# The first stage of a four-layer encoder: the norm's vectors on SyncE's queue, the third block's split between the squares, the sums over partitions inside group two

## The chip, the cores and the metric

The kernel runs on one core of a Trainium2 chip. The time is the device time of one execution in microseconds (us); lower is better. Engines are named as in the profile: PE (TensorE, matrix multiplications; PEld is its load of weights), DVE (VectorE), ACT (ScalarE), POOL (GpSimd) and SP (SyncE, which here only issues DMAs). L81 is line 81 of the kernel's file.

## The reference

Four layers on a sequence of 256 rows of 1024 numbers. Every layer is two half-step feed-forward networks with a token mixer between them (attention, convolution, Fourier, gated linear attention, one a layer). Only the first feed-forward network is touched by the change:

```python
def _rmsnorm(x, g):
    xf = x.astype(F32)
    y = xf * lax.rsqrt(jnp.mean(xf * xf, axis=-1, keepdims=True) + EPS)
    return (y * g.astype(F32)).astype(x.dtype)

def _swiglu(h, w1, w3, w2):
    return (jax.nn.silu(h @ w1) * (h @ w3)) @ w2

    h = x
    for i in range(DEPTH):
        h = h + 0.5 * _swiglu(_rmsnorm(h, norm_g[i, 0]), ffn_w1[i, 0], ffn_w3[i, 0], ffn_w2[i, 0])
        ...
```

`w1` and `w3` are 1024 x 2816, `w2` is 2816 x 1024, all float32.

## The kernel before

**Layout.** The activations stand transposed: 1024 features on partitions, in four tiles `h0` to `h3` of 128 x 2 x 256 (two groups of 128 features, 256 positions each). The weights come in **blocks** of 1 MB (128 x 2048), in the order in which they are used: block 0 is the first 256 columns of `w1`, block 1 those of `w3`, block 2 the next 256 columns of `w1`, block 3 those of `w3`, and so on. Four `raw` buffers take the loads, four `w` buffers what is made of them.

**Exact products.** Every operand is split into a high part that TensorE takes exactly and a low part. `split_block` (L160) does it for a block: ACT copies `raw` to the high part (L167, 128 x 2048), DVE subtracts (L170), and then the next load is issued into the `raw` buffer that has come free. `split` (L634) does it for smaller pieces (ACT L635, DVE L636). `wide` (`mm` at L81) multiplies: for each of the eight k (128 features) and each half c of the 256 columns a matmul of 256 columns and one of 512. A block used against all of x is so 32 matmuls.

**Groups.** A feed-forward network works through 11 pairs of blocks; I call the 64 matmuls on blocks 0 and 1 **group one**, the 32 on block 2 **group two** and the 32 on block 3 **group three**. `w1` blocks accumulate in two banks of PSUM, PA (`A0`, `A1`), `w3` blocks in two others, PB (`A2`, `A3`). Before a bank may be started anew, what stands in it is read: ACT copies one half (`parts`, L466) and DVE adds the other (`add`, L471). So group two may start only when `sl0`, group one's sum in PA, is read, and group three only when `br0` in PB is read and block 3 is split.

**The norm.** `normed` (L295) multiplies `h` by the gains only (vectors in `cols`, one small load) and splits the result into `x`; the factor 1/sqrt(mean of squares) is applied after the products (`times_r`). For that `square` (L314) sums squares into `acc`: ACT squares each `h` tile (L320, L328; the two `sq` buffers alternate, so the third `sq` waits until DVE has added the first), DVE adds (L355), folds the two halves (L335), and splits the result into `R` high (ACT L340) and low (DVE L341). `stats(True)` (L400) sums over partitions with two matmuls of a matrix of ones (**the sums**), and DVE makes the reciprocal root: L410, then L367, L368 and three Newton steps of L371 to L373, given out one after the other by `steps.pop(0)()`.

**Order.** Nothing is scheduled automatically: each engine executes its instructions in the order of the code, and waits on semaphores where it needs another engine's result. In `setup` (L196) POOL issues the load of `cols`; SP issues, for each j, the load of `h` tile j and of slice j of blocks 0 and 1, then blocks 2 and 3 and a small constant. At most eight loads of SP are outstanding, since their semaphores are reused. Then ACT and DVE make x and the splits slice by slice, then come the four `square` calls, the last of which calls `split_block` for block 2 after the fold. The first network (`first` in `ffn`) alternates between PA and PB, two k at a time, in all of group one, then makes the sums, then group two.

Of the kernel before, what the change touches and what calls it, by code (L numbers as in the profile page):

```python
# [38 lines left out]
class Enc:  # L39
# [156 lines left out]
    def setup(self):  # L196
        nc, a = self.nc, self.a
        self.perm = self.stages[0][1] == 0
        cols = self.const.tile([128, sum(n for _, n in COLS)], F32, name="cols")
        nc.gpsimd.dma_start(cols, a["cols"])  # L200
        names = [(*k, c) for k, n in COLS for c in range(n)]
        self.cols = {k if k[0] == "n" else (k[0], k[-1]): (cols, i) for i, k in enumerate(names)}

        self.h = [self.hp.tile([128, 2, 256], F32, name=f"h{j}") for j in range(4)]
        first = range(2 if self.stages[0][0] == "ffn" else 0)
        for b in first:
            self.raw[b] = self.sb(self.wp, [128, 2048], F32, "raw", NR)
            self.wsp[b] = self.pair(self.wp, [128, 2048], "w", NW)
        self.ndma = self.nsplit = len(first)
        for j in range(4):  # L210
            nc.sync.dma_start(self.h[j], a["x"][j])
            s = slice(512 * j, 512 * j + 512)
            for b in first:
                nc.sync.dma_start(self.raw[b][:, s], self.blocks[b][2][:, s])
        while self.ndma < NR:
            self.dma_block()
        self.ident = self.const.tile([128, 128], F32, name="ident")
        nc.sync.dma_start(self.ident, a["c_ident"])
        st = self.open_stage()
        one = self.sb(self.ev, [128, 128], F32, "one")  # L220
        nc.vector.memset(one, 1.0)
        self.ones_r = self.const.tile([128, 128], F32R, name="ones")
        nc.gpsimd.tensor_copy(self.ones_r, one)
        nc.scalar.activation(one[:, 0:1], one[:, 0:1], AF.Copy)
        self.ones = f32(self.ones_r)
        self.acc = self.hp.tile([128, 2, 256], F32, name="acc")
        self.begin_close()
        for j in range(4):
            self.normed(j)
            s = slice(512 * j, 512 * j + 512)  # L230
            for b in first:
                self.split(self.raw[b][:, s], self.wsp[b][:, :, s])
        for b in first:
            del self.raw[b]
        while self.ndma < NR + len(first):
            self.dma_block()
        for j in range(4):
            self.square(j, before_split=self.split_block)
        self.pend = NW - self.nsplit
        self.close_stage(st)  # L240

# [69 lines left out]
            nc.vector.tensor_scalar(y[:, 1], h[:, 1], g[1], None, ALU.mult)  # L311
            self.xn[j] = y

    def square(self, j, h=None, before_split=None):  # L314

        nc = self.nc
        h = self.h[j] if h is None else h
# [14 lines left out]
        if j == 3:  # L332
            self.flush_acc()
            if self.row_norm():
                nc.vector.tensor_tensor(self.acc[:, 0], self.acc[:, 0], self.acc[:, 1], ALU.add)  # L335
            if before_split:
                before_split()
            if self.row_norm():
                hi, lo = self.nsq = [self.sb(self.hp, [128, 256], F32R, "R", 2) for _ in range(2)]
                nc.scalar.activation(hi, self.acc[:, 0], AF.Copy)  # L340
                nc.vector.tensor_tensor(lo, self.acc[:, 0], f32(hi), ALU.subtract)  # L341
# [101 lines left out]
    def ffn(self, l, s):  # L443
        nc = self.nc
# [6 lines left out]
        PA, PB = (self.two(up_half, n) for n in range(2))  # L451

        def up(w, P, ks=range(8)):
            for k in ks:
                for c in range(2):
                    self.wide(P, c, w[:, :, :, 128 * c:128 * c + 128], k, self.xk(k), k == 0, k == 7)

        def take_up(n, i, P):
            up(self.take((n, i)), P)
            self.done()  # L460
# [23 lines left out]

        first = self.nstage == 0
        wa, wb = self.take(("w1", 0)), self.take(("w3", 0))
        cuts = [range(2 * n, 2 * n + 2) for n in range(4)] if first else [range(4), range(4, 8)]
        for n, ks in enumerate(cuts):
            if n == len(cuts) - 1:
                if not first:  # L490
                    self.pump(1)
                up(wa, PA, ks[:2])
                if first:
                    break
                steps = self.stats(True)
                up(wa, PA, ks[2:])
            else:
                up(wa, PA, ks)
                up(wb, PB, ks)
        self.done()  # L500
        sl0 = parts(PA, "sl")
        add(sl0, PA)
        up(wb, PB, ks)
        self.done()
        if first:
            steps = self.stats(True)
        held = self.pend - 2
        steps.pop(0)()
        br0 = parts(PB, "br")
# [3 lines left out]
        steps.pop(0)()  # L513
        self.pump(1)
        for i in range(1, NG):
            take_up("w1", i, PA)
            sl = parts(PA, "sl")
            if i == 1:
                self.pump(1, between=lambda: (add(sl, PA), times_r(sl0), times_r(sl)))
# [34 lines left out]
        w = self.take(("w2",))  # L554
# [8 lines left out]
        for p in range(NP):  # L563
# [3 lines left out]
            w = self.take(("w2", 1, p))  # L567
# [1072 lines left out]
```

## Time and profile before

| | us |
|---|---|
| median of 3 runs | 1934.15 |
| lowest, highest | 1933.92, 1937.98 |
| the profiled execution, its own time | 1937.17 |
| its span (first to last instruction) | 1935.0 |
| PE busy in the span | 1906.1 (99%) |
| DVE busy | 1397.5 (72%) |
| ACT busy | 995.4 (51%) |

The span is what the rows below divide; the time of an execution is some 2 us longer. A busy PE is not one at its peak, but idle time of PE is time in which it waits. The trace's rows give start and duration in us from the span's start; in square brackets stands how long the engine was idle before and whose result ended that.

### The profile page before, as it was taken

The numbers are of one execution on the slowest core, as the hardware profiler recorded it, in microseconds if no ns is written. First come the engines' busy times: TensorE is split into PE (matmuls) and PEld (weight loads), VectorE is DVE, ScalarE is ACT, GpSimd is POOL, SyncE is SP. The second block draws the span as 40 slices with busy tenths as digits, with TensorE's granted clock in tenths as the row PEclk, the third lists the DMA queues.
The fourth block names the chain that finished last, engine by engine and source line by source line (L and its number), as shares of the span: only waits on it lengthen the run. The fifth ranks groups of instructions, "written<-read, shape, count | busy, mean of one in ns | idle before, by whom it ended". The sixth has DMA issues, their size and how long they took to land.

```text
span 1935.0 us, 29203 instructions
## 1 busy us (share of the span) xinstructions
PE 1906.1 (99%) x12272; PEld 1683.3 (87%) x12272; DVE 1397.5 (72%) x1850; ACT 995.4 (51%) x1273; POOL 35.0 (2%) x55
## 2 busy tenths in 40 slices
PE   7999999999999999899999999999999999999998
PEld 6888999888888898788888889988888888998886
DVE  7776567876687767787668776687777766768774
ACT  6554444655455544555545544555445455756452
POOL 0000000000040000000000000000000000000000
PEclk9999999999999999899999999999999999999999
DMA  7655533465445543245545544365546553335550
GB/s 264 219 194 193 188 131 131 153 217 196 174 164 212 194 162 144 79 163 216 196 174 196 195 176 164 133 226 183 183 168 220 201 196 111 131 130 193 199 196 22
DMA packets 48644, 338.10 MB, mean 175 GB/s; under 512 B 5568, under 2 KB 5744, under 8 KB 8192
## 3 DMA queue, kind: packets, MB, share of 16 engines
q1 hardware_dynamic: 47952, 335.11, 48.3%
q8 instruction: 96, 1.57, 0.3%
q0 software_dynamic: 560, 1.12, 0.2%
q14 instruction: 36, 0.29, 0.0%
HBM read 335.16 MB, written 1.05 MB: 174 GB/s over the span
## 4 chain that ended last, share of the span: by engine, by line
PE 92%; DVE 5%; ACT 2%; DMA 1%; issue 1%; SPq 0%; DVEq 0%; ACTq 0%
PE B L81 50%; PE A L81 41%; DVE w L170 1%; ACT w L167 1%; DVE zc L765 1%; DMA raw<-in_ffn_w_dram 0%; PE A L84 0%; DMA h<-in_x_dram 0%; ACT zc L880 0%; PE B L84 0%; DVE h L279 0%; DVE acc L355 0%; DVE x L304 0%; DVE sl L474 0%; ACT x L302 0%
## 5 line engine op out<-in xcount | busy, mean ns | idle before, releaser
L170 DVE TENSOR_TENSOR w<-raw,w 128x2048 fp32r<-128x2048 f32 x315 | 720.4, 2293 | 289.7 <-ACT w L167 289.4
L167 ACT ACTIVATE w<-raw 128x2048 fp32r<-128x2048 f32 x315 | 598.8, 1909 | 109.0 <-PE A L81 47.4
L81 PE MATMUL B<-x,w 128*128 128x256 f32 (+1 forms) x3968 | 643.5, 322 | 1.4 <-DVE sl L471 1.2
L81 PEld LDWEIGHTS B<-x,w 128*128 128x128 f32 x3968 | 571.5, 190 | 71.1 <-issue 5.5
L81 PE MATMUL A<-x,w 128*128 128x256 f32 x3008 | 522.4, 335 | 10.9 <-DVE w L636 7.3
L81 PEld LDWEIGHTS A<-x,w 128*128 128x128 f32 x3008 | 455.5, 189 | 74.9 <-DVE w L636 7.3
L81 PE MATMUL B<-g,w 128*128 128x256 f32 (+1 forms) x1408 | 251.1, 336 | 0.3 <-DVE w L170 0.2
L81 PE MATMUL A<-g,w 128*128 128x256 f32 (+1 forms) x1408 | 250.3, 336 | 0.0
L81 PEld LDWEIGHTS B<-g,w 128*128 128x128 f32 x1408 | 216.5, 187 | 32.2 <-DVE g L636 0.5
L81 PEld LDWEIGHTS A<-g,w 128*128 128x128 f32 x1408 | 216.6, 187 | 31.4
L635 ACT ACTIVATE g<-br 128x512 fp32r<-128x512 f32 x88 | 55.6, 632 | 252.9 <-DVE br L480 252.9
L474 DVE TENSOR_TENSOR sl<-sl,R 128x512 f32<-128x512 f32 x176 | 121.9, 696 | 2.5
L636 DVE TENSOR_TENSOR g<-br,g 128x512 fp32r<-128x512 f32 x88 | 61.1, 695 | 61.4 <-ACT g L635 61.4
L302 ACT ACTIVATE x<-h,cols 128x256 fp32r<-128x256 f32 x88 | 39.9, 501 | 68.3 <-DVE h L279 49.0
L466 ACT ACTIVATE br<-B 128x256 f32<-128x256 f32 x88 | 30.3, 385 | 76.3 <-PE B L81 76.3
L477 ACT ACTIVATE sl<-sl 128x512 f32<-128x512 f32 x88 | 55.0, 627 | 24.5 <-DVE sl L474 24.4
L466 ACT ACTIVATE br<-A 128x256 f32<-128x256 f32 x88 | 30.2, 384 | 71.5 <-PE A L81 71.4
L81 PE MATMUL B<-w,x 128*128 128x256 f32 (+1 forms) x504 | 62.6, 284 | 0.0
L81 PEld LDWEIGHTS B<-w,x 128*128 128x128 f32 x504 | 61.3, 191 | 0.4 <-issue 0.3
L480 DVE TENSOR_TENSOR br<-sl,br 128x512 f32<-128x512 f32 x88 | 60.7, 690 | 0.5
L466 ACT ACTIVATE sl<-A 128x256 f32<-128x256 f32 x88 | 29.8, 377 | 53.1 <-PE A L81 53.1
L466 ACT ACTIVATE sl<-B 128x256 f32<-128x256 f32 x88 | 29.9, 378 | 51.5 <-PE B L81 51.1
(293 smaller groups left out, 1088.9 us busy)
## 6 DMA issues: line engine op xcount, KB each, us to landing
raw<-in_ffn_w_dram SPq DMA_DIRECT2D x262, 1024.0 KB, 4.8
raw<-in_attn_w_qk_dram SPq DMA_DIRECT2D x12, 1024.0 KB, 4.8
raw<-in_conv_w_pw_dram SPq DMA_DIRECT2D x12, 1024.0 KB, 4.8
raw<-in_gla_w_in_dram SPq DMA_DIRECT2D x12, 1024.0 KB, 4.8
raw<-in_attn_w_v_dram SPq DMA_DIRECT2D x6, 1024.0 KB, 4.8
raw<-in_fnet_w_dram SPq DMA_DIRECT2D x4, 1024.0 KB, 4.8
raw<-in_gla_w_o_dram SPq DMA_DIRECT2D x4, 1024.0 KB, 4.7
raw<-in_ffn_w_dram SPq DMA_DIRECT2D x8, 256.0 KB, 6.1
```

What stands on the lines that cost most here:

```text
L81: return self.nc.tensor.matmul(out, lhsT, rhs, start=start, stop=stop, skip_group_check=True)
L167: self.nc.scalar.activation(w[:, 0], raw, AF.Copy)
L170: (eng or self.nc.vector).tensor_tensor(w[:, 1], raw, f32(w[:, 0]), ALU.subtract)
L302: nc.scalar.activation(xh[:, c], h[:, c], AF.Copy, scale=g[c])
L466: nc.scalar.activation(t[:, c], P[c][:, 1], AF.Copy)
L474: nc.vector.tensor_tensor(t, t, self.Rb(), ALU.mult)
L477: nc.scalar.activation(t, t, AF.Silu)
L480: nc.vector.tensor_tensor(br, sl, br, ALU.mult)
L635: self.nc.scalar.activation(p[:, 0], src, AF.Copy)
L636: self.nc.vector.tensor_tensor(p[:, 1], src, f32(p[:, 0]), ALU.subtract)
L765: nc.vector.scalar_tensor_tensor(o, x, w, o, ALU.mult, ALU.add)
```

## The change

Four edits, all in the first stage (the same code serves the other stages, whose order does not change):

- `cols` is loaded by SP, ahead of its other loads, and no longer by POOL.
- `split_block` for block 2 stands between the second and the third `square` call, and no longer in the fourth one.
- In group one, k 0 to 3 still alternate between PA and PB; then come k 4 to 7 of PA in one go, and then those of PB.
- The two matmuls of the sums no longer stand between group one and group two but in the middle of group two, after its first four k.

```diff
--- before.py
+++ after.py
@@ -197,7 +197,7 @@
         nc, a = self.nc, self.a
         self.perm = self.stages[0][1] == 0
         cols = self.const.tile([128, sum(n for _, n in COLS)], F32, name="cols")
-        nc.gpsimd.dma_start(cols, a["cols"])
+        nc.sync.dma_start(cols, a["cols"])
         names = [(*k, c) for k, n in COLS for c in range(n)]
         self.cols = {k if k[0] == "n" else (k[0], k[-1]): (cols, i) for i, k in enumerate(names)}
 
@@ -235,7 +235,9 @@
         while self.ndma < NR + len(first):
             self.dma_block()
         for j in range(4):
-            self.square(j, before_split=self.split_block)
+            if j == 2:
+                self.split_block()
+            self.square(j)
         self.pend = NW - self.nsplit
         self.close_stage(st)
 
@@ -311,7 +313,7 @@
             nc.vector.tensor_scalar(y[:, 1], h[:, 1], g[1], None, ALU.mult)
             self.xn[j] = y
 
-    def square(self, j, h=None, before_split=None):
+    def square(self, j, h=None):
 
         nc = self.nc
         h = self.h[j] if h is None else h
@@ -333,8 +335,6 @@
             self.flush_acc()
             if self.row_norm():
                 nc.vector.tensor_tensor(self.acc[:, 0], self.acc[:, 0], self.acc[:, 1], ALU.add)
-            if before_split:
-                before_split()
             if self.row_norm():
                 hi, lo = self.nsq = [self.sb(self.hp, [128, 256], F32R, "R", 2) for _ in range(2)]
                 nc.scalar.activation(hi, self.acc[:, 0], AF.Copy)
@@ -484,26 +484,28 @@
 
         first = self.nstage == 0
         wa, wb = self.take(("w1", 0)), self.take(("w3", 0))
-        cuts = [range(2 * n, 2 * n + 2) for n in range(4)] if first else [range(4), range(4, 8)]
-        for n, ks in enumerate(cuts):
-            if n == len(cuts) - 1:
-                if not first:
-                    self.pump(1)
-                up(wa, PA, ks[:2])
-                if first:
-                    break
-                steps = self.stats(True)
-                up(wa, PA, ks[2:])
-            else:
-                up(wa, PA, ks)
-                up(wb, PB, ks)
+        if first:
+            for n in range(2):
+                for P, w in ((PA, wa), (PB, wb)):
+                    up(w, P, range(2 * n, 2 * n + 2))
+            up(wa, PA, range(4, 8))
+        else:
+            for P, w in ((PA, wa), (PB, wb)):
+                up(w, P, range(4))
+            self.pump(1)
+            up(wa, PA, range(4, 6))
+            steps = self.stats(True)
+            up(wa, PA, range(6, 8))
         self.done()
         sl0 = parts(PA, "sl")
         add(sl0, PA)
-        up(wb, PB, ks)
+        up(wb, PB, range(4, 8))
         self.done()
         if first:
+            wa = self.take(("w1", 1))
+            up(wa, PA, range(4))
             steps = self.stats(True)
+            up(wa, PA, range(4, 8))
         held = self.pend - 2
         steps.pop(0)()
         br0 = parts(PB, "br")
@@ -513,7 +515,10 @@
         steps.pop(0)()
         self.pump(1)
         for i in range(1, NG):
-            take_up("w1", i, PA)
+            if first and i == 1:
+                self.done()
+            else:
+                take_up("w1", i, PA)
             sl = parts(PA, "sl")
             if i == 1:
                 self.pump(1, between=lambda: (add(sl, PA), times_r(sl0), times_r(sl)))
```

ACT from its first square on, before, then after (`w_167` and `w_159` are block 2, `w_269` and `w_301` block 3, `A_69` and `A_70` the banks of PA, `sl` group one's sum):

```order
L320 ACTIVATE acc<-h_81 128x512
L328 ACTIVATE sq_157<-h_82 128x512
L328 ACTIVATE sq_160<-h_83 128x512
L328 ACTIVATE sq_163<-h_84 128x512
L167 ACTIVATE w_167<-raw_101 128x2048
L340 ACTIVATE R_172<-acc 128x256
L466 ACTIVATE sl_236<-A_69 128x256
```

```order
L322 ACTIVATE acc<-h_81 128x512
L330 ACTIVATE sq_157<-h_82 128x512
L167 ACTIVATE w_159<-raw_101 128x2048
L330 ACTIVATE sq_165<-h_83 128x512
L330 ACTIVATE sq_168<-h_84 128x512
L340 ACTIVATE R_172<-acc 128x256
L466 ACTIVATE sl_228<-A_69 128x256
```

Block 2's copy stands two squares earlier.

DVE from the last slice of block 1 on, before, then after (`B_73` is the bank of the sums):

```order
L636 TENSOR_TENSOR w_88<-raw_87,w_88 128x512
L355 TENSOR_TENSOR acc<-acc,sq_157 128x512
L355 TENSOR_TENSOR acc<-acc,sq_160 128x512
L355 TENSOR_TENSOR acc<-acc,sq_163 128x512
L335 TENSOR_TENSOR acc<-acc 128x256
L170 TENSOR_TENSOR w_167<-raw_101,w_167 128x2048
L341 TENSOR_TENSOR R_173<-acc,R_172 128x256
L471 TENSOR_TENSOR sl_236<-sl_236,A_69 128x256
L471 TENSOR_TENSOR sl_236<-sl_236,A_70 128x256
L410 TENSOR_SCALAR R_249<-B_73 128x256
```

```order
L641 TENSOR_TENSOR w_88<-raw_87,w_88 128x512
L170 TENSOR_TENSOR w_159<-raw_101,w_159 128x2048
L355 TENSOR_TENSOR acc<-acc,sq_157 128x512
L355 TENSOR_TENSOR acc<-acc,sq_165 128x512
L355 TENSOR_TENSOR acc<-acc,sq_168 128x512
L337 TENSOR_TENSOR acc<-acc 128x256
L341 TENSOR_TENSOR R_173<-acc,R_172 128x256
L471 TENSOR_TENSOR sl_228<-sl_228,A_69 128x256
L471 TENSOR_TENSOR sl_228<-sl_228,A_70 128x256
L410 TENSOR_SCALAR R_265<-B_73 128x256
```

Block 2's subtraction has moved from behind the fold to ahead of all three additions; the rows from L341 on stand as before.

PE around the sums, before, then after (`x_9_116` holds k 0 and 1, `x_10_125` k 2 and 3, `x_11_134` k 4 and 5, `x_12_143` k 6 and 7; `w_88` is block 1):

```order
L81 MATMUL A_72<-x_12_143,w_88 128x256
L81 MATMUL A_72<-x_12_143,w_88 128x512
L81 MATMUL B_73<-R_172,ones 128x256
L81 MATMUL B_73<-R_173,ones 128x256
L81 MATMUL A_69<-x_9_116,w_167 128x256
L81 MATMUL A_69<-x_9_116,w_167 128x512
```

```order
L81 MATMUL A_70<-x_10_125,w_159 128x256
L81 MATMUL A_70<-x_10_125,w_159 128x512
L81 MATMUL B_73<-R_172,ones 128x256
L81 MATMUL B_73<-R_173,ones 128x256
L81 MATMUL A_69<-x_11_134,w_159 128x256
L81 MATMUL A_69<-x_11_134,w_159 128x512
```

The sums stand behind the first 16 of group two's 32 matmuls, and group two's first matmul follows group one's last.

## Rows read from the trace of the kernel before

**Rows 1.** The page: busy us (share of span) and instructions of PE

```profile
PE 1906.1 (99%) x12272; PEld 1683.3 (87%) x12272; DVE 1397.5 (72%) x1850; ACT 995.4 (51%) x1273; POOL 35.0 (2%) x55
```

**Rows 2.** Waits of PE, whole span: us in total, times, longest us

```profile
PE A L81 <- DVE w L636: 7.3, 1, 7.3
...
PE B L81 <- DVE R L341: 1.4, 1, 1.4
...
PE A L81 <- DVE w L170: 1.1, 1, 1.1
```

**Rows 3.** Timeline of PE, 0 to 60 us: start, duration, engine, line, what

```profile
7.33 12.97 PE L81 MATMUL A<-x,w 128*128 128x256 f32 x64 [7.33 <-DVE w L636]
...
21.79 0.39 PE L81 MATMUL B<-R,ones 128*128 128x256 f32 x1 [1.38 <-DVE R L341]
22.12 5.82 PE L81 MATMUL A<-x,w 128*128 128x256 f32 x32
29.07 17.22 PE L81 MATMUL A<-x,w 128*128 128x256 f32 x96 [1.13 <-DVE w L170]
```

**Rows 4.** Timeline of DVE, 0 to 60 us

```profile
15.91 2.29 DVE L355 TENSOR_TENSOR acc<-acc,sq 128x512 f32<-128x512 f32 x3 [0.35 <-ACT sq L328]
18.23 0.43 DVE L335 TENSOR_TENSOR acc<-acc 128x256 f32<-128x256 f32 x1
19.11 2.29 DVE L170 TENSOR_TENSOR w<-raw,w 128x2048 fp32r<-128x2048 f32 x1 [0.45 <-ACT w L167]
21.32 0.42 DVE L341 TENSOR_TENSOR R<-acc,R 128x256 fp32r<-128x256 f32 x1
21.66 0.75 DVE L471 TENSOR_TENSOR sl<-sl,A 128x256 f32<-128x256 f32 x2
22.32 0.42 DVE L410 TENSOR_SCALAR R<-B 128x256 f32<-128x256 f32 x1
...
26.73 2.28 DVE L170 TENSOR_TENSOR w<-raw,w 128x2048 fp32r<-128x2048 f32 x1
...
32.40 0.74 DVE L471 TENSOR_TENSOR sl<-sl,A 128x256 f32<-128x256 f32 x2
```

**Rows 5.** Timeline of ACT, 0 to 60 us

```profile
5.12 0.91 ACT L302 ACTIVATE x<-h,cols 128x256 fp32r<-128x256 f32 x2 [2.64 <-DMA cols<-in_cols_dram]
...
15.26 1.14 ACT L328 ACTIVATE sq<-h 128x512 f32<-128x512 f32 x2
16.64 0.63 ACT L328 ACTIVATE sq<-h 128x512 f32<-128x512 f32 x1 [0.24 <-DVE acc L355]
17.17 1.90 ACT L167 ACTIVATE w<-raw 128x2048 fp32r<-128x2048 f32 x1
18.98 0.40 ACT L340 ACTIVATE R<-acc 128x256 fp32r<-128x256 f32 x1
```

**Rows 6.** Timeline of SP's queue, 0 to 10 us: issues of loads

```profile
0.74 0.39 SPq L211 DMA_DIRECT2D h<-in_x_dram  x1
...
7.58 1.72 SPq L158 DMA_DIRECT2D raw<-in_ffn_w_dram  x2
```

**Rows 7.** DMA issues, 0.7 to 1.17 us (first `h`): count, KB, us to landing

```profile
h<-in_x_dram SPq DMA_DIRECT2D x1, 256.0 KB, 2.8
```

**Rows 8.** DMA issues, 1.2 to 1.3 us (first slice of block 0, `cols`)

```profile
raw<-in_ffn_w_dram SPq DMA_DIRECT2D x1, 256.0 KB, 3.1
cols<-in_cols_dram POOLq DMA_DIRECT2D x1, 84.0 KB, 3.8
```

**Rows 9.** DMA issues, 7.5 to 8.0 us (block 2)

```profile
raw<-in_ffn_w_dram SPq DMA_DIRECT2D x1, 1024.0 KB, 9.1
```

**Rows 10.** Busy us (x instructions) PE, PEld, DVE, ACT, POOL; PE's clock, DMA share, GB/s

```profile
8.00:10.00 2.00, 2.00 (x7) 1.67 (x7) 1.63 (x4) 1.36 (x3) 0.00 (x0) 1.00 1.06 398
14.00:16.00 2.00, 2.00 (x13) 1.72 (x12) 0.79 (x2) 1.80 (x4) 0.00 (x0) 1.00 1.03 430
...
812.00:814.00 2.00, 1.64 (x7) 1.44 (x8) 0.76 (x2) 2.00 (x3) 0.00 (x0) 0.65 0.80 328
814.00:816.00 2.00, 2.00 (x11) 2.00 (x11) 1.62 (x1) 2.00 (x2) 0.00 (x0) 0.50 0.31 131
816.00:818.00 2.00, 2.00 (x19) 2.00 (x18) 2.00 (x2) 0.14 (x1) 0.00 (x0) 1.00 0.23 33
```

**Rows 11.** Timeline of PE, 808 to 821 us

```profile
812.29 8.99 PE L81 MATMUL A<-zs,w 128*128 128x256 f32 x58 [2.35 <-ACT zs L635]
```

## The prediction

> **What bounds the kernel now.** I read the page first: PE is busy 99% of the span [rows 1], so time is lost only where PE waits, or runs slowly. The waits of PE over the whole span are few, and three of the longest lie in the stage that the change touches [rows 2]: 7.3 us until the first slice of block 0 is split, 1.4 us until the low part of `R` is there for the sums, 1.1 us until block 3 is split. The timeline of PE places them [rows 3]: group one runs from 7.33 for 12.97 us without a wait, the second matmul of the sums begins at 21.79, group two at 22.12, group three at 29.07, and from there 96 matmuls follow without a gap. What matters is therefore one number: when group three starts. After that PE has no wait in these rows, and every microsecond by which the start moves stays in the time.
>
> Next, who sets these starts. Block 0's loads were there early; what held ACT until 5.12 was `cols` [rows 5], issued by POOL and landed 3.8 us after its issue [rows 8]. DVE's rows show the second and third wait [rows 4]: the subtraction of block 2 occupies it from 19.11 for 2.29 us, then the low part of `R` (21.32), then the two additions that empty PA (from 21.66), and group two starts at 22.12 as the first of them ends: block 2 itself was split by 21.40. The chain L410 to the block-3 subtraction (22.32 to 26.73 + 2.28 = 29.01) is DVE's without a pause, and group three starts at its end. So DVE, not PE, carries this stage between 19 and 29 us, and group three starts 29.07 - 22.32 = 6.75 us after L410.
>
> **cols on SP's queue.** The first `h` lands 2.8 us after its issue at 0.74 [rows 6, 7]. With `cols` ahead of it, it is issued one SP issue (0.39 us [rows 6]) later, and lands at about 3.9 to 4.0; `cols`, a third of its size, lands by then. ACT's first product starts near 4.0 in place of 5.12. Block 0's first slice landed 3.1 us after its issue at about 1.2 [rows 8], so near 4.7 with the same delay, when ACT is through with x. From ACT's 5.12 to PE's 7.33 it is 2.2 us, so PE starts near 6.2: 1.1 us earlier (bounds: 0.7, with one more issue time lost, and 1.2, what 3.9 instead of 5.12 leaves). Group one, without a wait before, then ends near 19.1, if its data keep ahead; with PA's k 4 to 7 in one go the last slice of block 0 is needed 8 matmuls earlier, some 1.4 us (8 x 0.18, below). I cost that at nothing, since a stall there would only use up part of the wait that comes next, and the same wait makes PE's earlier start worth nothing.
>
> Loads behind `cols`: the later ones run with the DMA engines full (share 1.03 to 1.06 [rows 10]), and the bytes are the same, so I take block 2's landing as unchanged: issue 7.58 [rows 6] + 9.1 [rows 9] = 16.7. Ends: 0.4 later (the issue time), 0.8 earlier (where ACT would no longer be waiting). The Trainium skill ("Trainium Kernel Development and Optimization", Key Constraints) says that DMAs of SP, ACT and POOL queues run on the same 16 engines, and that issuing from several only saves the sequencer's issue time. That speaks against this edit: by it the issue time is simply lost, +0.4 us on the sum below.
>
> **Block 2's split between the squares.** ACT is through with the second square at about 15.26 + 0.6 = 15.9 [rows 5], before block 2 is there. So ACT now waits for the load, and behind it are queued two squares, on which `R` rests. Step by step, with durations of rows 4 and 5: the copy 16.7 to 18.6 (1.90); the subtraction to 20.9 (2.29); the first addition to 21.6, upon which the third square may overwrite its buffer; three additions (2.29 with their waits) to 23.2; fold (0.43) 23.6; high part on ACT (0.40) 24.0; low part (0.42) 24.5; the first of the two PA additions (0.75 for two) 24.85. Before, the same addition ended at 22.1. The additions used to run while ACT copied block 2; now DVE stands idle meanwhile (15.91 - 0.35 = 15.6 to 18.6) and does them afterwards. Block 2 is split 0.5 us earlier, which nobody waits for.
>
> **The sums in group two.** Group two follows group one directly in PE's order, but its first matmul starts PA anew, and PA is emptied by `add`, which on DVE stands behind the low part of `R`. So group two starts at 24.85 in place of 22.12, 2.7 later, whatever PE gained at the front. Then 16 matmuls: 17.22/96 = 0.18 each [rows 3], 2.9 us, to 27.75. Only now come the sums. In the old order L410 came 0.53 us after the second of them began; the first adds 0.2 (between its weight load and its length). So L410 starts at 28.4 and not at 22.32: 6.1 later. Group two's other half (2.9) covers part of that for PE, but DVE's chain of 6.75 us to group three is unbroken, the same instructions in the same order. Group three starts at 28.4 + 6.75 = 35.15. **Sum without the clock: +6.1 us.** Behind that nothing changes: PA's next sum `sl` is added on DVE 32.40 - 29.07 = 3.3 us after group three starts [rows 3, 4], within its 5.7 us.
>
> **What the waits do to PE's clock.** PE would idle from 19.1 to 24.85 (5.7 us) and from the end of group two, about 31.1, to 35.15 (4.0 us), in place of 1.4 and 1.1. At 812.29 a wait of 2.35 us ends [rows 11] and the granted clock drops to 0.50, the 1.2 GHz level [rows 10]: 11 matmuls in 2 us there, 19 in the next 2 us at 1.00. At the start too, after 7.33 us of nothing, 7 matmuls lie in 8 to 10 us against 13 in 14 to 16 us, though the column reads 1.00. After the waits of 1.4 and 1.1 us the rates are full: 32 matmuls in 5.82 us right after the first [rows 3]. Both new waits exceed the 2.35 us, so I let both cost a stretch at half clock. The stretch at 812 is some 3.5 us long (0.65 in the first window, of which 1.6 us ran, 0.50 in the second). At 11 to 19 it loses 42%: 1.5 us. I take 1.6 for each; the ends are 0 and 2.4 (all of a group's 5.8 us at the lower rate). The first delays the sums (they stand behind 16 matmuls that run slowly), the second falls on group three, which PE has no slack to regain. The Trainium skill ("TensorE: Matmul & The Clock Gate", Why this matters for your kernels) advises against PE idle gaps above about 3 us between bursts, since the clock then halves. By it too both waits cost, and the second, for which I have only one row, is the likelier; the row at 812 shows a shorter wait doing it.
>
> **Total:** 6.1 + 1.6 + 1.6 = 9.3 us. The profiled execution took 1937.17 us with a span of 1935.0; these become 1946.5 and 1944.3. The median of the runs is 1934.15, 3.0 below the profiled one, so the forecast for a median is 1934.15 + 9.3 = 1943.45, rounded 1943.5.
>
> **Rivals.**
> 1. *One clock drop only* (the second wait ends in full clock): +7.7, 1941.8. For it: the second wait is the shorter, and only one row shows such a drop.
> 2. *No drop*: +6.1, 1940.2; with block 2 landing 0.8 us earlier 1939.4. Against it: the row at 812.
> 3. *Longer slow stretches, later loads*: +0.4 and 2.4 for each drop: 6.1 + 0.4 + 4.8 = 11.3, 1945.5.
> 4. *Faster*: the point that decides is whether PA is emptied by the end of group one, near 19.1. Were the two additions done by then, PE would gain 1.1 at the start and lose both waits, 1.4 and 1.1 [rows 2]: -3.6, 1930.5. For it: PE's order is indeed freed of the wait for `R`, and the sums are no longer between the groups. Against it: DVE's order puts these additions behind L341, which needs all squares, and the last of them cannot be added before 23 us while the copy waits for a load that lands at 16.7.
> 5. *Within the measurement*: the mechanism holds but costs little: the load lands early and no clock drops (1939.4), and the chain of rows 4 runs 1.5 us shorter than its rows say, about 1938. Against it: these rows are back to back, with nothing to save.
>
> **How the numbers follow.** Something like 0.2% (3.9 us) is what a measurement of this kernel can tell from no change; the three runs of before differ by 4.1. Both drops 0.52, one 0.2, none 0.08, longer stretches 0.1, within 0.2% 0.07, faster 0.03. Slower by over 0.2% (above 1938.0) are the first four: 0.90. The forecast is the likeliest case, 1943.5. The range leaves out rivals 4 and 5 and what runs scatter beyond: from 1939.4 (none, load early) to 1946.5 (longer stretches and 1.0 of scatter).
>
> **What the next profile would show.** PE's first matmul near 6.2; group one's end near 19; group two waiting for DVE's L471 (not for the split of block 2) until about 24.9; the sums at 28 to 30; group three waiting for block 3's subtraction until 35 to 37; the granted clock at 0.50 after the first of these waits and probably after the second; from there on every row later by the same amount. I am wrong if group two starts before 22.1, if ACT's copy of block 2 starts much before 16.7, or if L410 runs ahead of group two. An end that is later by about 6 with a clock at 1.00 would mean that only the clock term failed.

## The result, and the profile after

The changed kernel takes 1945.72 us (median of 5 runs, 1943.57 to 1948.5) against 1935.22 us of the kernel before (median of 5 on the same chip, 1933.92 to 1937.98): 1.0054 times as long, with an interval of 1.0043 to 1.0066, or 10.5 us more. The forecast was 1943.5, 9.3 us more. The profiled execution took 1948.5 us with a span of 1946.4.

PE in the first 60 us of the changed kernel; the columns and names are those of [rows 3]:

```profile
6.29 14.06 PE L81 MATMUL A<-x,w 128*128 128x256 f32 x64 [6.29 <-DVE w L641]
25.84 4.45 PE L81 MATMUL A<-x,w 128*128 128x256 f32 x16 [5.49 <-DVE sl L471]
30.13 0.40 PE L81 MATMUL B<-R,ones 128*128 128x256 f32 x2
30.36 2.94 PE L81 MATMUL A<-x,w 128*128 128x256 f32 x16
37.31 19.58 PE L81 MATMUL A<-x,w 128*128 128x256 f32 x96 [4.01 <-DVE w L170]
```

Group one starts 1.0 us earlier than in [rows 3] and ends at the same time: its 64 matmuls take 14.06 and not 12.97 us. Then PE stands for 5.49 us until DVE's L471 has emptied the first bank of PA. The first 16 matmuls of group two take 4.45 us, the next 16 only 2.94. Group three starts at 37.31 (29.07 before), and its row is 2.36 us longer than 17.22.

ACT and DVE of the changed kernel in the same stretch, the rows that answer to [rows 4, 5]:

```profile
17.65 1.92 ACT L167 ACTIVATE w<-raw 128x2048 fp32r<-128x2048 f32 x1 [0.79 <-DMA raw<-in_ffn_w_dram]
...
22.58 0.63 ACT L330 ACTIVATE sq<-h 128x512 f32<-128x512 f32 x1 [2.50 <-DVE acc L355]
24.58 0.42 ACT L340 ACTIVATE R<-acc 128x256 fp32r<-128x256 f32 x1 [1.36 <-DVE acc L337]
```

```profile
19.60 2.29 DVE L170 TENSOR_TENSOR w<-raw,w 128x2048 fp32r<-128x2048 f32 x1 [3.05 <-ACT w L167]
21.81 2.28 DVE L355 TENSOR_TENSOR acc<-acc,sq 128x512 f32<-128x512 f32 x3
24.12 0.43 DVE L337 TENSOR_TENSOR acc<-acc 128x256 f32<-128x256 f32 x1
25.02 0.42 DVE L341 TENSOR_TENSOR R<-acc,R 128x256 fp32r<-128x256 f32 x1 [0.48 <-ACT R L340]
25.37 0.75 DVE L471 TENSOR_TENSOR sl<-sl,A 128x256 f32<-128x256 f32 x2
30.56 0.42 DVE L410 TENSOR_SCALAR R<-B 128x256 f32<-128x256 f32 x1 [4.45 <-PE B L81]
...
34.98 2.28 DVE L170 TENSOR_TENSOR w<-raw,w 128x2048 fp32r<-128x2048 f32 x1
```

ACT now waits for block 2's load, DVE stands for 3.05 us until ACT's copy is through, and the three additions (2.28 us), which before ran ahead of this copy's end (15.91 to 18.20), come after it. Block 2 is split at 21.89, but the wait that ends last at group two is L471, 3.5 us later. L410 waits 4.45 us for the sums, which stand behind the 16 slow matmuls; from there to group three it is 6.75 us, as before.

The granted clock, by windows of the changed kernel (busy us, instructions in brackets, for PE, PEld, DVE, ACT and POOL, then PEclk, share of the DMA engines, GB/s):

```profile
8.00:10.00 2.00, 2.00 (x8) 1.71 (x8) 1.57 (x3) 1.10 (x3) 0.00 (x0) 1.00 0.97 330
10.00:12.00 2.00, 2.00 (x8) 1.71 (x7) 1.29 (x3) 1.91 (x4) 0.00 (x0) 1.00 1.08 399
12.00:14.00 2.00, 2.00 (x13) 1.72 (x13) 2.00 (x5) 1.95 (x5) 0.00 (x0) 1.00 1.02 378
...
26.00:28.00 2.00, 2.00 (x7) 1.71 (x8) 0.12 (x1) 2.00 (x3) 0.00 (x0) 0.50 0.19 78
28.00:30.00 2.00, 2.00 (x11) 1.77 (x10) 0.00 (x0) 1.68 (x1) 0.00 (x0) 0.77 0.06 20
...
38.00:40.00 2.00, 2.00 (x7) 1.65 (x7) 1.97 (x3) 0.00 (x0) 0.00 (x0) 0.50 0.75 238
40.00:42.00 2.00, 2.00 (x8) 1.67 (x7) 2.00 (x5) 0.00 (x0) 0.00 (x0) 0.50 1.22 356
42.00:44.00 2.00, 2.00 (x11) 1.74 (x10) 2.00 (x2) 1.24 (x2) 0.00 (x0) 0.85 0.65 274
```

After either wait the clock is at 0.50, the 1.2 GHz level, with 7 or 8 matmuls in 2 us where 13 or 14 go at full rate. At the start 8 matmuls lie in a window until 12 us, although the column reads 1.00 (the last section says why).

**Where the loss ends.** Executions of one kernel scatter: 25 of the kernel before on one chip lie between 1931.4 and 1939.0 us. So I also compare a place soon behind the first stage: the start of the row after a short PE wait in the next one. Timeline of PE, 345 to 364 us, the kernel before and then the changed one:

```profile
351.87 12.34 PE L81 MATMUL B<-x,w 128*128 128x256 f32 x68 [1.02 <-DVE sl L471]
```

```profile
362.47 1.78 PE L81 MATMUL B<-x,w 128*128 128x256 f32 x9 [0.94 <-DVE sl L471]
```

It is 10.60 us later. The two differences above account for it: 8.24 (start of group three) + 2.36 (length of its row) = 10.60. No other gain or loss is left over up to there, and the times of the runs say the same (10.5). I call this row's shift against the kernel before the **shift at 352**; it is the measure that the experiments are read by, with the times beside it.

What scatters behind it shows in the traces. Near 1630 us, in code that no kernel here changes, one row of 48 matmuls takes 7.35 to 7.85 us in nine of the twelve traces and 6.02 in the other three (split_late, bank_first, fill_second). The kernel before, with a window of its clock, then split_late:

```profile
1631.70 7.55 PE L81 MATMUL B<-x,w 128*128 128x256 f32 x48
```

```profile
1630.00:1632.00 2.00, 2.00 (x3) 0.49 (x3) 0.00 (x0) 0.19 (x1) 0.00 (x0) 0.50 0.54 225
```

```profile
1635.53 6.02 PE L81 MATMUL B<-x,w 128*128 128x256 f32 x48
```

The clock falls there to 0.50 in the nine, and stays at 1.00 in the three. From the row at 352 to the end of this one the three take 1283.8 to 1284.3 us, the kernel before 1287.2 and the changed one 1288.3. The profiled execution of the kernel before is one of the slow nine, and with 1937.17 us above its median; a shift is free of this, a difference of medians is not.

### The profile page after: what moved, and what is told of

The parts are those of the page before. It is cut to its first block, busy times and chain, and to the rows that moved or that the text cites. A ratio compares the mean times of both kernels' runs of the same rounds, so it can differ in the third digit from the quotient of the medians.

```text
span 1946.4 us, 29202 instructions
## 1 busy us (share of the span) xinstructions
PE 1911.7 (98%) x12272; PEld 1688.4 (87%) x12272; DVE 1397.5 (72%) x1850; ACT 996.2 (51%) x1273; POOL 34.4 (2%) x54
## 4 chain that ended last, share of the span: by engine, by line
PE 92%; DVE 5%; ACT 2%; DMA 1%; issue 1%; SPq 0%; DVEq 0%; ACTq 0%
PE B L81 49%; PE A L81 42%; DVE w L170 1%; ACT w L167 1%; DMA raw<-in_ffn_w_dram 1%; DVE zc L770 1%; PE A L84 0%; DVE acc L355 0%; ACT zc L885 0%; PE B L84 0%; DVE h L281 0%; DVE x L306 0%; DVE sl L474 0%; ACT x L304 0%; DVE nRu L372 0%
```

## The experiments

Theory: three parts of the loss can be separated. PA is emptied late, since L471 stands behind a longer chain on DVE; the sums stand behind half of group two; and behind both new waits PE's clock is halved for a while. `cols` does nothing. The rivals: `cols` on SP delays the loads; or the late split of block 2 itself is what PE waits for; or the clock costs little. In the table, "group two" and "group three" are the starts of their first matmuls, "96" is the length of the row that begins with group three, "shift" the shift at 352; for the kernel before and the changed one the trace is the one shown.

| kernel | median us (runs) | ratio, interval | group two | L410 | group three | 96 | shift |
|---|---|---|---|---|---|---|---|
| before | 1935.22 (5) | | 22.12 | 22.32 | 29.07 | 17.22 | |
| changed | 1945.72 (5) | 1.0054, 1.0043 to 1.0066 | 25.84 | 30.56 | 37.31 | 19.58 | +10.60 |
| changed_again | 1947.05 (5) | 1.005, 1.0036 to 1.0064 | 24.06 | 28.94 | 35.69 | 19.67 | +9.08 |
| cols_alone | 1936.15 (11) | 1.0001, 0.9993 to 1.001 | 22.32 | 22.51 | 29.26 | 16.92 | -0.10 |
| cols_on_pool | 1945.46 (7) | 1.0041, 1.0027 to 1.0056 | 24.55 | 30.50 | 37.25 | 18.48 | +9.44 |
| sums_between | 1938.56 (11) | 1.0016, 1.0007 to 1.0025 | 25.48 | 25.72 | no wait | | +3.10 |
| split_late | 1941.74 (6) | 1.0027, 1.0016 to 1.0038 | 21.93 | 25.31 | 32.07 | 19.52 | +5.26 |
| bank_first | 1938.07 (9) | 1.0024, 1.0014 to 1.0034 | 21.36 | 24.88 | 31.63 | 18.49 | +3.81 |
| filled | 1943.09 (5) | 1.0042, 1.003 to 1.0055 | 25.15 | 28.47 | 35.24 | 16.92 | +5.88 |
| fill_first | 1943.99 (5) | 1.0041, 1.0028 to 1.0055 | 24.78 | 28.04 | 34.80 | 18.50 | +7.00 |
| fill_second | 1942.2 (5) | 1.0035, 1.0023 to 1.0048 | 25.70 | 30.95 | 37.71 | 16.92 | +8.34 |
| split_before_chain | 1933.6 (11) | 0.9992, 0.9984 to 1.0001 | 21.82 | 25.21 | no wait | | -1.38 |

The ratios are taken against runs of the kernel before on the same chip (medians 1935.9 for cols_alone, cols_on_pool, sums_between and split_late; 1936.03 for changed_again, fill_first and fill_second; 1934.84 for bank_first, filled and split_before_chain).

**cols_alone: the kernel before with the first edit only.**

```diff
-        nc.gpsimd.dma_start(cols, a["cols"])
+        nc.sync.dma_start(cols, a["cols"])
```

> The kernel before with the first edit alone: cols is loaded by SP, ahead of its other loads. Chain theory (DVE's order and the loads set groups two and three): PE starts near 6.3, but block 2 lands 1.0 us later, as in the changed kernel (17.6 instead of 16.65), and so group two starts near 23.1 and group three near 30.1; the time is +1.0 us against before (1936), or +2.5 if the longer wait before group two halves the clock. Rival (PE's earlier start counts): group three starts near 28.1, time -1.0 (1934).

No difference: 1.0001, shift -0.10. Its PE:

```profile
6.30 13.35 PE L81 MATMUL A<-x,w 128*128 128x256 f32 x64 [6.30 <-DVE w L636]
21.99 0.38 PE L81 MATMUL B<-R,ones 128*128 128x256 f32 x1 [1.91 <-DVE R L341]
22.32 5.91 PE L81 MATMUL A<-x,w 128*128 128x256 f32 x32
```

The 1.03 us gained at the front go into a slower group one (13.35 us for 12.97) and a longer wait for the sums (1.91 for 1.38). The later landing that I expected after the first trace did not show: block 2 lands at 16.9 us (16.7 before), and ACT's copy of it, which does not wait for it here, starts at 17.37 (17.17 before).

**cols_on_pool: the changed kernel without the first edit** (the line above, back on POOL).

> The changed kernel with cols back on POOL. Chain theory: PE starts at 7.3 again, but block 2 lands near 16.65 and everything from ACT's copy of it on is 1.0 earlier: group two near 24.85, group three near 36.3, time -1.0 against the changed kernel (1944.7). Rival (the landing is not set by cols): same landing as the changed kernel, 17.6, and no difference, or +1 for the later start.

1.0041, shift +9.44: as slow as the changed kernel, within what its two traces differ by (+10.60, +9.08), and not 1.0 us faster as expected.

```profile
24.55 5.49 PE L81 MATMUL A<-x,w 128*128 128x256 f32 x16 [2.94 <-DVE sl L471]
29.83 0.63 PE L81 MATMUL B<-R,ones 128*128 128x256 f32 x2
...
37.25 18.48 PE L81 MATMUL A<-x,w 128*128 128x256 f32 x96 [3.92 <-DVE w L170]
```

Block 2 came 1.3 us earlier than in the changed kernel's trace (ACT's copy at 16.35 for 17.65), and group two started 1.3 earlier; but its 16 matmuls ran at half clock throughout (0.50 in all of 24 to 30 us), so L410 stood at 30.50 again. In this execution, what an earlier load gave, the clock took. Two of the seven runs took only 1938.66 and 1939.63 us, the other five 1945.4 to 1947.7. None of the changed kernel's ten came below 1943.5. No trace was kept of the two, so what they were spared is open.

**sums_between: the changed kernel with the sums ahead of group two.**

```diff
-            up(wa, PA, range(4))
             steps = self.stats(True)
-            up(wa, PA, range(4, 8))
+            up(wa, PA)
```

> The changed kernel with the sums back between group one and group two. Chain theory: group two still starts near 25.9 (PA's banks), but L410 near 26.0 instead of 30.56, so DVE's chain ends near 32.8 and group three starts at 33 to 33.7, as group two (slowed) ends; the second wait and its stretch at half clock are gone. Time +4 to +5 against before, 1939.5 to 1940. Rival (the place of the sums is not what costs, the wait for the banks and the clock are): within 2 us of the changed kernel, 1944 to 1946.

1.0016, or 2.7 us more, where 4 to 5 were expected; shift +3.10.

```profile
24.73 0.95 PE L81 MATMUL B<-R,ones 128*128 128x256 f32 x2 [4.62 <-ACT R L340]
25.48 23.91 PE L81 MATMUL A<-x,w 128*128 128x256 f32 x128
```

The row of 24.73 is both sums; the second begins at 25.10, 3.3 us later than the 21.79 of [rows 3], and group two follows 3.36 us later than before. That is what the block's split ahead of the additions costs on DVE. PE is at half clock from 24.9 to 28.3 us, so the 128 matmuls take 23.91 us, 0.87 more than the 5.82 and 17.22 of [rows 3]. Group three follows without a wait, which saves the 1.13 us of before: 3.36 + 0.87 - 1.13 = 3.10. So with the sums left in their old place the change costs some 3 us, and the sums' place brings the rest.

**split_late: the changed kernel with the split back behind the fold** (`square` gets its `before_split` again).

> The changed kernel with block 2's split back behind the fold. Chain theory: the additions run again while ACT copies block 2, so group two starts near 23.1 (22.1 + 1.0 for the later loads), L410 at 26.5 to 28, group three at 33.2 to 34.8, after a second wait of some 4 us with its stretch at half clock; +6 to +8 against before, 1941.5 to 1943.5, 2.5 to 4 less than the changed kernel. Rival (the split's place costs nothing, the banks are emptied late for another reason): group two stays near 25.8, time 1945.7.

1.0027, or 5.8 us more (6 to 8 expected, with a later load that did not come); shift +5.26.

```profile
21.93 3.10 PE L81 MATMUL A<-x,w 128*128 128x256 f32 x16 [2.48 <-DVE sl L471]
24.87 0.40 PE L81 MATMUL B<-R,ones 128*128 128x256 f32 x2
...
32.07 19.52 PE L81 MATMUL A<-x,w 128*128 128x256 f32 x96 [3.97 <-DVE w L170]
```

Group two starts only 0.2 us earlier than before, although it no longer waits for the sums: L471 ends its wait. L410 is 3.0 us later (25.31 for 22.32), group three 3.0, and the row of 96 is 2.3 longer, at half clock from 32 to 36 us: 5.3. Here the wait of 2.48 us did not slow what followed it: 16 matmuls in 3.10.

**bank_first: the changed kernel with PA emptied before the last two squares are added.**

```diff
-        for j in range(4):
-            if j == 2:
-                self.split_block()
+        for j in range(2):
             self.square(j)
+        self.flush_acc()
+        self.split_block()
...
         add(sl0, PA)
+        if first:
+            for j in range(2, 4):
+                self.square(j)
         up(wb, PB, range(4, 8))
```

> The changed kernel in which DVE empties PA's banks (L471) right after block 2's subtraction, ahead of the last two additions of squares, the fold and the split of R. Bank theory (group two waits for PA alone): group two starts near 22.3 instead of 25.84; the sums then wait for R, L410 near 26.0 to 27.5, group three near 33 to 34, with a second wait near 4 us and its slow stretch; time 1941 to 1942.5. Rival (group two needs something else of the norm's chain): its start stays near 25.8.

1.0024, shift +3.81. Its DVE, then its PE:

```profile
18.68 2.29 DVE L170 TENSOR_TENSOR w<-raw,w 128x2048 fp32r<-128x2048 f32 x1 [2.05 <-ACT w L167]
20.89 0.74 DVE L471 TENSOR_TENSOR sl<-sl,A 128x256 f32<-128x256 f32 x2
21.55 1.48 DVE L355 TENSOR_TENSOR acc<-acc,br 128x512 f32<-128x512 f32 x2
```

```profile
21.36 3.09 PE L81 MATMUL A<-x,w 128*128 128x256 f32 x16 [1.28 <-DVE sl L471]
...
31.63 18.49 PE L81 MATMUL A<-x,w 128*128 128x256 f32 x96 [3.97 <-DVE w L170]
```

This tells the bank from the split: block 2's subtraction is still ahead of the last two additions, L471 now too, and group two starts 2.7 to 4.5 us earlier than in the changed kernel's traces, at full clock. (The first addition has moved ahead of the subtraction as well, into time in which DVE waited for ACT's copy anyway.) Counted from the start of that copy, which differs by the load, it is 4.64 us (21.36 - 16.72) for 8.19. The loss that is left is the sums' place (L410 2.56 us later) and the slow stretch behind the second wait (1.3).

**filled, fill_first, fill_second: PE kept busy in the waits** by matmuls of 512 columns into an unused bank, 20 ahead of group two and 14 ahead of group three; the second and the third kernel have only the one or the other.

```diff
+    def fill(self, n):
+        for _ in range(n):
+            self.mm(self.dbank(3), self.ones_r, self.xn[0][:, 0].rearrange("p c n -> p (c n)"), True, True)
...
+            self.fill(20)
             up(wa, PA, range(4))
...
+            if first and i == 1:
+                self.fill(14)
             take_up("w3", i, PB)
```

> The changed kernel with matmuls that nobody uses in the two waits, into a bank that is free then: 20 ahead of group two, 14 ahead of group three (of 512 columns, about 4.7 and 3.3 us), so that PE idles under 1 us in each. They add work that the output does not use. Theory of the clock (stretches at 1.2 GHz behind the two waits cost 1.5 and 2.4 us): both groups run at full clock, group two's first half takes 2.8 instead of 4.3 us, L410 comes near 29.0, group three near 35.8, 96 matmuls in 17.2 us; time -4 against the changed kernel, 1941.5 to 1942. Rival (the clock costs nothing that counts): 1945.7 or more.

> The changed kernel with 20 unused matmuls in the wait ahead of group two alone. Clock theory: group two's first 16 matmuls take 3.1 us instead of 4.5 to 5.5, L410 and group three come 1.5 to 2.5 us earlier, the second wait (4 us) and its stretch at half clock stay: -1.5 to -2.5 us against the changed kernel. Rival (the chain on DVE hides the slow matmuls): no difference.

> The changed kernel with 14 unused matmuls in the wait ahead of group three alone. Clock theory: group two is slow as in the changed kernel, but the 96 matmuls from group three on take 17 us instead of 18.5 to 19.6: -1.5 to -2.5 us against the changed kernel. Rival (what PE loses there it regains in later waits): no difference.

PE of filled, of fill_first, and of fill_second:

```profile
19.69 4.74 PE L81 MATMUL B<-x,ones 128*128 128x512 f32 x20
25.15 3.05 PE L81 MATMUL A<-x,w 128*128 128x256 f32 x16 [0.72 <-DVE sl L475]
...
31.05 3.36 PE L81 MATMUL B<-x,ones 128*128 128x512 f32 x14
35.24 16.92 PE L81 MATMUL A<-x,w 128*128 128x256 f32 x96 [0.82 <-DVE w L170]
```

```profile
24.78 2.99 PE L81 MATMUL A<-x,w 128*128 128x256 f32 x16
...
34.80 18.50 PE L81 MATMUL A<-x,w 128*128 128x256 f32 x96 [3.97 <-DVE w L170]
```

```profile
25.70 4.97 PE L81 MATMUL A<-x,w 128*128 128x256 f32 x16 [6.29 <-DVE sl L475]
...
37.71 16.92 PE L81 MATMUL A<-x,w 128*128 128x256 f32 x96 [0.82 <-DVE w L170]
```

Each filler takes away the slow stretch behind it and not the other one: 16 matmuls in 2.99 to 3.05 us for 4.45 to 5.49, 96 in 16.92 for 18.48 to 19.67. (In fill_first the fillers end only after L471, which holds group two up by some 0.5 us: it starts 8.65 us after ACT's copy and not 8.19.) With both, the shift is +5.88 and the clock reads 1.00 in every window between 18 and 40 us: that is the loss without the clock, forecast as 6.1. By the medians filled is 8.2 us slower than before, not 5.9. Its profiled execution is the median one (1943.09) and one of those with the slow stretch near 1630; against the profiled one of the kernel before, which has it too, the times differ by 5.9 as the shift does. For the same reason the medians of fill_first and fill_second, 3.1 and 4.9 us below changed_again's, say less than their shifts, 2.1 and 0.7 below its: fill_second's trace has no slow stretch near 1630, changed_again's has one. (Of the shifts, fill_second's is raised by its load: ACT's copy starts 1.65 us later than in changed_again.)

**changed_again: the changed kernel once more,** beside the two fillers.

> The changed kernel once more, as the partner on the same chip for the two runs that fill one wait each: +9.5 to +11 us against before, two stretches at half clock behind waits of 3 to 5.5 us and of 4 us.

1.005, shift +9.08.

```profile
24.06 4.61 PE L81 MATMUL A<-x,w 128*128 128x256 f32 x16 [4.03 <-DVE sl L471]
...
35.69 19.67 PE L81 MATMUL A<-x,w 128*128 128x256 f32 x96 [4.01 <-DVE w L170]
```

The 1.5 us less than in the first trace come from the load: ACT's copy of block 2 starts at 15.87 and not at 17.65, and group two 8.19 us after it in both. The same 8.2 us lie between the two starts in cols_on_pool (16.35, 24.55), filled (16.96, 25.15) and fill_second (17.52, 25.70). The times do not show this: the median is 11.0 us above before's.

**split_before_chain: a version without the losses.** `cols` on POOL and the split of block 2 after the fold, as before; group one's order and the sums in the middle of group two, as changed; and on DVE the two additions that empty PA ahead of `R`, and block 3's split and the emptying of PB ahead of L410's chain.

```diff
         add(sl0, PA)
+        if first:
+            self.hilo()
+            self.pump(1)
         up(wb, PB, range(4, 8))
         self.done()
         if first:
+            br0 = parts(PB, "br")
+            add(br0, PB)
...
```

(`hilo` is the split of the sum of squares into `R`, taken out of `square`; `pump(1)` splits block 3. The edits that put the first two changes back, and the `if not first` around the old place of `br0`, are left out here.)

> A kernel built on what the traces show: cols on POOL, block 2's split behind the fold as before, the changed order of group one, PA's banks emptied ahead of R's low part, block 3 split and PB's banks emptied ahead of the sums' chain (L410 and the Newton steps), the sums inside group two. Chain theory: group two starts near 21.8 and group three follows it near 27.7 without a wait, 1.4 us before the 29.07 of the kernel before; time 1933.8 against 1935.2. Rival (DVE has no slack later and PE waits in the next groups instead): no difference, 1935 to 1936.5.

0.9992, with an interval of 0.9984 to 1.0001; shift -1.38. Its PE, then its DVE:

```profile
21.82 3.09 PE L81 MATMUL A<-x,w 128*128 128x256 f32 x16 [1.39 <-DVE sl L474]
...
24.98 19.96 PE L81 MATMUL A<-x,w 128*128 128x256 f32 x112
```

```profile
22.34 2.28 DVE L170 TENSOR_TENSOR w<-raw,w 128x2048 fp32r<-128x2048 f32 x1
24.55 0.74 DVE L474 TENSOR_TENSOR br<-br,A 128x256 f32<-128x256 f32 x2
25.21 0.42 DVE L413 TENSOR_SCALAR R<-B 128x256 f32<-128x256 f32 x1
```

Group three follows group two without a wait: the second wait of PE before (1.13 us) is gone, in the trace. With the sums inside group two the chain of the norm may start 2.9 us later than before without harm, as long as block 3's split does not stand behind it. The shift is that wait and the 0.30 us by which group two starts earlier; the runs' interval still includes no change, so I call it a kernel that is no slower, not one that is shown to be faster. It has group one's new order too, as split_late has, and in both group two starts 0.2 to 0.3 us earlier than before: that order, which was not run by itself, costs nothing that shows.

## Why the prediction held, and which terms were off

**The wait for the bank: right.** Group two waits for L471, not for block 2's split. bank_first shows it by moving L471 ahead of the last additions. It started at 25.84 and not at 24.85; the whole difference is block 2's load, which came about 1 us later than I took (copy at 17.65, not 16.7). From the copy on I had 24.85 - 16.7 = 8.15 us, and the five traces named above have 8.2.

**The landing: right on average, too firm for one execution.** I let 16.7 stand with ends of -0.8 and +0.4. In the kernels with `cols` on SP where ACT waits for the load, its copy starts at 15.87, 16.13, 16.72, 16.96, 17.24, 17.52 and 17.65: mean 16.87, so 0.8 before my 16.7 to 0.95 after it; one trace with `cols` on POOL has 16.35. The scatter is between executions. SP issues block 2 at 8.16 to 9.48 us in the nine traces with `cols` on its queue, and at 7.58 to 8.23 in the three without, so the issue moves, mostly by more than the 0.4 us that I gave it; the landing does not follow, since the load then takes 7.2 to 9.3 us from issue to landing, for 9.1 before. The Trainium skill ("Trainium Kernel Development and Optimization", Key Constraints) says that the queues share the same engines and that only issue time is to be had. No run here can show whether that issue time was lost in the end: in cols_alone the wait for the sums swallows whatever is won or lost at the front.

**PE's early start is worth nothing: right, for one reason more.** PE started at 6.29 (forecast 6.2). I let group one end 1.1 us earlier, at 19.1, and the wait use that up. In the changed kernel's trace group one ended where it did before, since its slow rate lasted until 12 us, 1.4 us longer than before; in split_late, where it lasted until 9.9, group one took 12.90 us from 6.56. Either way the wait behind it takes up the difference.

**The sums behind half of group two: right.** L410 to group three is 6.75 to 6.77 us in every trace that has the wait. At full clock L410 came 3.3 us after group two's start (filled 3.32, fill_first 3.26, split_late 3.38), forecast 3.55.

**The clock: right in kind, the second term too small.** That the clock would fall behind both waits I took from one row, the wait of 2.35 us at 812 us. It did, but the same trace has two more stretches at 0.50 that I did not look at, at 792 us behind waits of at most 1.48 us and near 1630 behind none, and a wait of 2.48 us in split_late brought no stretch. So the ground was weaker than the forecast made it; that waits of 2.9 us and more bring a stretch each time is shown by the runs, and was not by that row. I took 1.6 us for each stretch, with 2.4 as the end. The first: L410 stood 4.72, 4.88, 5.25 and 5.95 us after group two's start in the changed kernel, changed_again, fill_second and cols_on_pool, against 3.3: +1.4, +1.6, +1.9 and +2.6. The second: 96 matmuls took 18.48 to 19.67 us against 16.92: +1.6 to +2.7. This is the mis-sized term, and it is the length that was missed, not the rate: my row at 812 us [rows 10, 11] showed a stretch of 3.5 us at a loss of 42%, and behind 37.31 PE works at 0.50 for 5.3 us, in changed_again for 6.0.

**The sum, once more.** Of the changed kernel's 10.60: L471 late 3.72 (25.84 - 22.12), the sums behind 16 matmuls 3.1, their slow rate 1.4, the second slow stretch 2.4. Against 9.3 that is +1.0 by the landing, -0.4 by the first 16 matmuls and +0.8 by the second stretch. Undone one at a time, the parts leave +3.1 (sums back) and +5.3 (split back); together they cost more, 9.1 to 10.6 against 8.4. With both, the first slow stretch lies ahead of the sums and delays L410 by 1.4 to 2.6 us, and the 1.13 us saved in sums_between are not saved.

**The rivals.** One drop or none (1941.8, 1940.2) fall: both waits slow what follows, in both traces of the changed kernel. Longer stretches and later loads (+11.3) are not told from the forecast (+9.3): the first trace (+10.6) and both differences of medians (+10.5, +11.0) lie nearer to that rival, the second trace (+9.1) nearer to the forecast. Its 2.4 us fits the second stretch better than my 1.6; its later load is not there on average. Giving it 0.1 against 0.52 was too bold. The faster case failed where the prediction put its deciding point: PA was emptied at 25.8, not by the end of group one.

## What to carry to other kernels

When a matmul is moved ahead of a wait, look up what the next matmuls need besides that wait: here a bank that DVE empties late, so the one wait was only exchanged for another, and the result whose wait was avoided came later. On an engine that works in the order of the code, short instructions that set free a bank or the next operand belong ahead of a long serial chain and ahead of anything that waits for a load (bank_first and split_before_chain). In this kernel a wait that kept PE idle for 2.9 us or more was followed by slow matmuls each time, at a cost of 0.9 to 2.7 us. Where another engine's chain stands behind these matmuls, that cost moves the whole chain. And compare kernels at a place soon behind the change, beside the medians: a slow stretch elsewhere in the program, 3 to 5 us here, can lie in the one profile and not in the other.

## What the runs showed of the hardware

**The price of a slow stretch follows the time that PE works in it, not the length of the wait.** By the clock levels that the traces hold, PE worked at 0.50 for 3.1 us behind group two's start in the changed kernel (wait 5.49), 3.4 in changed_again (4.03), 4.2 in fill_second (6.29) and 5.9 in cols_on_pool (2.94), and L410 came 1.4, 1.6, 1.9 and 2.6 us late. Behind group three's start 3.4 us cost 1.6 (cols_on_pool, bank_first, fill_first), 5.1 to 5.3 cost 2.6 to 2.7 (split_late, changed) and 6.0 cost 2.75 (changed_again). That is some 0.45 to 0.5 us for each us at the lower level, the 1.2 GHz one.

**The length of the wait alone does not tell whether the clock falls.** Waits of 2.35 us at 812 us [rows 10, 11] and of 1.77 to 1.92 us at the same place in other traces (1.92 in the changed kernel's, at 822.91) were followed by 0.50; 1.59 us there in split_before_chain, 1.91 us in cols_alone (ahead of the sums) and 2.48 us in split_late were not. Near 1630 us the clock fell in nine traces with PE busy throughout, while it alternated pairs of matmuls on 17 partitions with six on 128. The Trainium skill ("TensorE: Matmul & The Clock Gate", Why this matters for your kernels) advises against PE idle for more than about 3 us between bursts; by it the wait at 812 would have been free, and the rows have 0.50 after it; the waits of 3.9 us and more agree with it, unless fillers stand in them. What decides in the shorter waits is left open.

**Unrelated matmuls keep the clock.** Fillers that nobody reads, over most of the wait, were enough, with at most 0.8 us of idle time left behind them.

**The column of the clock is no reading at the start of a run.** It reads 1.00 from 8 to 12 us in the changed kernel while 8 matmuls lie in each 2 us, as in [rows 10] between 8 and 10; 13 lie in the window from 12 on. The trace holds no clock level ahead of 11.87 us there, and none ahead of 10.47 us in the kernel before; the 1.00 printed for that time is no reading. In the traces looked at in steps of 0.5 us (first level at 9.43 us in fill_second, 9.90 in split_late, 13.37 in cols_on_pool) the matmuls speed up where the first level stands, from 3 or 4 in a step to 4 or 5. So the first matmuls ran slowly for 2.9 to 6.0 us, and an earlier start at that rate gains less than the time by which it is earlier.

**A small load on another queue.** The load of `cols` (84 KB) landed 2.0 us after its issue by SP as first load, against 3.8 us by POOL [rows 8]. ACT, which had waited for it until 5.12 us, then starts at 4.08 and waits for `h` instead; the time gains nothing by it (cols_alone).
